# A fused decoder layer on one core: the place of A21's plain product in the up units of the feed-forward

## The chip, the cores and the metric

The kernel runs on one core of a Trainium2 chip. The metric is the device time of one launch in microseconds, the median of three runs.

## What is computed

The reference is one inference step of a one-layer hybrid trunk: a mixer (gated linear attention, a gated linear recurrence and sliding-window attention side by side), cross-attention to a memory, and a feed-forward block, each added to the residual. It is done for 1024 prompt rows and for 8 sample rows. The change lies in the feed-forward block, with a width of 1024 and 4096 hidden features:

```python
def ffn(x, g, w1, w2):
    h = rmsnorm(x, g) @ w1
    return jnp.square(jax.nn.relu(h)) @ w2
...
xp = xp + ffn(xp, g_ffn[l], ffn_w1[l], ffn_w2[l])
...
xs = xs + ffn(xs, g_ffn[l], ffn_w1[l], ffn_w2[l])
```

## The kernel before, in words

Activations lie transposed, features on the partitions and the 1032 rows (1024 prompt, 8 sample) as columns, in three groups of 344. Every float32 operand of a product is split into a high and a low half, and a product is three matmuls for each block of 128 features: high by high, low by high, high by low (`terms`, L1938). `halves` makes the two: ScalarE writes the high half, VectorE subtracts it from the source (line L171 is the helper of every VectorE subtraction or addition, L161 of every ScalarE operation, L141 of every matmul).

**The up stage** multiplies by `ffn_w1`. Of its 16 column pairs, two are done plainly before, and 14 are *up units* (`up_unit`, L2037). A unit takes 256 hidden features, seen as a 2 by 2 array of weight blocks A11, A12, A21, A22. For the first two column groups it uses a scheme of seven products in place of eight: A11 and A12 with two blocks of the input, S2, S1, S4 and S3 (sums and differences of the blocks, by GpSimd, L1918) with sums of the input, and A22 with one more. The third column group gets the four plain products of A11, A12, A21, A22. So one weight operand has one or two products, each of 4 blocks x 3 terms = 12 matmuls of 344 columns: 11 products, 132 matmuls a unit.

The PSUM tiles are called `fa` (A11 and A12, first group), `fb` (S2), `fc` (S1), `fg` (S4), `fd` (S3, and A22 on top of it), and `fe` (the plain ones: one tile for A11 and A12, another for A21 and A22). The sums U = fb + p1 and V = fc + U lie in tile `gc`; the outputs of a unit lie in `hc`. Two cells of `hc` come from `fd`: the cell h11 is `fd` + V, read when S3's product alone is in it, and h10 is `fd` + U, read when A22's product has been added to it:

```python
elif i == S3:
    terms(bank(psC, "fd"), w, XOP[T3], True, False)
    with lift(LIFT_E):
        tt(h[1, 1], ps["fd"], V, ADD)
...
elif i == A21:
    terms(bank(psB, "fe"), w, XOP[GA][:4], True, False)
else:
    terms(ps["fd"], w, XOP[T4], False, True)
    terms(ps["fe"], w, XOP[GA][4:], False, True)
```

So TensorE may add A22's product to `fd` only after VectorE has read `fd` for h11.

**Order.** The order of the products in an up unit is that of the eight numbers in L1860: the loop runs i from 0 to 7, and `seq` gives `range(8)` for an up unit. The same numbers order the preparation of the operands: `prep` (L1921) makes the halves (tile `wop`) five products ahead (`LOOK`), in two alternating rings of three buffers each. At A11's preparation it also issues the next unit's weight load (tile `wraw`) and the four sums (tile `wsum`, one buffer each). Between the products, `bg_run(2)` and, from position 5 on, one entry of `slow` put in the storing of finished hidden features: halves into a ring of three buffers (tiles `hst` and `wsum`), subtractions in place (`hc`, `hpl`), and stores to memory (`hd`). In the last up unit, L2099 also issues loads of the down stage's operands at the positions of S1, S4 and S3. A scheduler with priorities then decides the order of the rows on each engine; `lift` gives a step more priority.

**The down stage** (`down_unit`, 16 units) multiplies by `ffn_w2` with the same scheme. Its order names the operands in `seq`, not by number.

Of the kernel before, what the change touches and what calls it, by code (L numbers as in the profile page):

```python
# [52 lines left out]
def trunk_step(ctx: ExitStack, tc: tile.TileContext, I: dict, O: list):  # L53
# [1803 lines left out]

    A11, S2, S1, A12, S4, A21, S3, A22 = range(8)  # L1860
    B11, T2, B21, T1, T3, B22, T4, GA = range(8)
    NPAIR, NPLAIN, NUNIT = DFF // 256, 2, DFF // 512
    HALF, QU, NOP = N // 2, N // 4, 7
# [533 lines left out]
```

## Time and profile before

| | |
|---|---|
| median of 3 runs | 1407.40 us (1407.39 to 1409.67) |
| the profiled execution | 1409.29 us, span of its records 1407.3 us |
| TensorE busy | 1326.3 us (94% of the span), granted clock 0.98 on the mean |
| VectorE, ScalarE, GpSimd busy | 1017.0, 686.8, 255.1 us |
| up units, from the first `fa` matmul to the first of the down stage | 748.72 to 1069.64 us |

Busy time is an average over stages. What the change is worth has to be read in the up stage, from the waits of TensorE there. Matmuls overlap in the records, so a matmul's row is longer than the step from one to the next. In the rows of a timeline the first number is the start in us from the span's start, the second the duration, and the bracket, where there is one, the idle time of the engine before it and what ended it.

### The profile page before, as it was taken

Reading aid. Unit: us, or ns where it says so; the run is one execution under the profiler, and the core shown is the slowest. Engines: PE = TensorE matmul, PEld = TensorE weight load, DVE = VectorE, ACT = ScalarE, POOL = GpSimd, SP = SyncE. Lnnn points to the kernel's source line nnn. Section 1 sums busy time; section 2 is a strip of 40 time slices with the busy share of each in tenths; the row PEclk is TensorE's granted clock in tenths of the full one; section 3 lists DMA queues with packets and bytes.
Section 4 is the critical chain, followed back from the end, with each engine's and each line's share of the span. In section 5 each row is a group of like instructions: output and inputs, shape, how many; then the busy total and the mean of one; then the engine's idle time right before and its main releaser. Section 6 shows DMA issues by size and latency. Waiting matters only on the chain.

```text
span 1407.3 us, 24488 instructions
## 1 busy us (share of the span) xinstructions
PE 1326.3 (94%) x9251; PEld 1219.1 (87%) x9251; DVE 1017.0 (72%) x1993; ACT 686.8 (49%) x1393; POOL 255.1 (18%) x245
## 2 busy tenths in 40 slices
PE   6999999999997989998999999998999999999998
PEld 4889888777876977887798999998999999999997
DVE  6276787668767673767798887887775577877775
ACT  5265464245476554645665666665665422222221
POOL 3001011400003101020014222242202223223310
PEclk9999999999998899998999999999999999999999
DMA  6114010211101453532243777674659989775624
GB/s 183 46 49 120 9 48 18 65 26 31 51 4 54 135 157 113 155 117 75 66 126 118 276 252 268 236 264 179 232 180 343 336 301 343 266 256 209 228 83 121
DMA packets 181021, 215.87 MB, mean 153 GB/s; under 512 B 26866, under 2 KB 114990, under 8 KB 180888
## 3 DMA queue, kind: packets, MB, share of 16 engines
q1 hardware_dynamic: 180264, 214.01, 45.0%
q8 instruction: 73, 1.20, 0.4%
q0 software_dynamic: 640, 0.30, 0.1%
q14 instruction: 44, 0.36, 0.1%
HBM read 145.28 MB, written 70.06 MB: 153 GB/s over the span
## 4 chain that ended last, share of the span: by engine, by line
PE 73%; DVE 14%; ACT 5%; DMA 3%; issue 3%; SPq 1%; POOL 0%; DVEq 0%; ACTq 0%; POOLq 0%
PE win L141 9%; PE a L141 7%; PE d L141 7%; PE c L141 7%; PE wo L141 6%; PE fe L141 4%; PE b L141 3%; PE fa L141 3%; PE fd L141 2%; PE v L141 2%; PE f L141 2%; PE gx L141 2%; PE fb L141 2%; PE fc L141 2%; PE wmo L141 2%
## 5 line engine op out<-in xcount | busy, mean ns | idle before, releaser
L1918 POOL TENSOR_TENSOR wsum<-wraw 128x512 f32<-128x512 f32 x60 | 81.4, 1357 | 408.0 <-DVE wop L171 374.5
L141 PE MATMUL win<-XL,wh 128*128 128x344 f32 x384 | 127.7, 333 | 0.0
L141 PE MATMUL win<-XH,wh 128*128 128x344 f32 x384 | 127.5, 332 | 0.2 <-ACT xy L161 0.2
L141 PE MATMUL win<-XH,wl 128*128 128x344 f32 x384 | 126.7, 330 | 0.0
L161 ACT ACTIVATE wop<-wraw 128x512 fp32r<-128x512 f32 x104 | 65.3, 628 | 118.5 <-PE b L141 31.3
L161 ACT ACTIVATE wop<-wsum 128x512 fp32r<-128x512 f32 x104 | 65.3, 628 | 110.5 <-PE d L141 29.8
L141 PE MATMUL fe<-XH,wop 128*128 128x344 f32 x448 | 117.4, 321 | 0.0
L161 ACT ACTIVATE wh<-ws 128x512 fp32r<-128x512 f32 x130 | 79.9, 626 | 75.0 <-DMA ws<-in_w_out_dram 21.2
L171 DVE TENSOR_TENSOR wop<-wraw,wop 128x512 fp32r<-128x512 f32 x104 | 93.5, 899 | 27.8 <-ACT wop L161 24.7
L171 DVE TENSOR_TENSOR wl<-ws,wh 128x512 fp32r<-128x512 f32 x130 | 93.0, 727 | 28.0 <-ACT wh L161 23.4
L171 DVE TENSOR_TENSOR wop<-wsum,wop 128x512 fp32r<-128x512 f32 x104 | 80.7, 776 | 17.4 <-ACT wop L161 15.0
L141 PEld LDWEIGHTS fe<-XH,wop 128*128 128x128 f32 x448 | 79.8, 189 | 0.0
L141 PEld LDWEIGHTS win<-XL,wh 128*128 128x128 f32 x384 | 73.1, 190 | 5.2 <-issue 3.9
L141 PEld LDWEIGHTS win<-XH,wl 128*128 128x128 f32 x384 | 73.3, 191 | 3.6 <-issue 2.7
L141 PEld LDWEIGHTS win<-XH,wh 128*128 128x128 f32 x384 | 73.2, 191 | 3.3 <-issue 1.9
L161 ACT ACTIVATE hc<-hc 128x344 f32<-128x344 f32 x126 | 59.9, 487 | 29.0 <-DVE hc L171 27.8
L141 PE MATMUL fe<-XL,wop 128*128 128x344 f32 x224 | 71.8, 321 | 0.0
L141 PE MATMUL a<-XH,wop 128*128 128x258 f32 x352 | 67.6, 283 | 0.0
L141 PE MATMUL wo<-XH,wh 128*128 128x344 f32 x192 | 64.3, 335 | 2.2 <-ACT wh L161 2.2
L141 PE MATMUL wo<-XH,wl 128*128 128x344 f32 x192 | 64.1, 334 | 1.0 <-DVE wl L171 0.9
L141 PE MATMUL wo<-XL,wh 128*128 128x344 f32 x192 | 63.0, 328 | 0.0
L141 PE MATMUL d<-XH,wop 128*128 128x258 f32 x320 | 60.8, 282 | 0.0
(543 smaller groups left out, 4109.4 us busy)
## 6 DMA issues: line engine op xcount, KB each, us to landing
hd<-hst SPq DMA_DIRECT2D x75, 516.0 KB
wraw<-in_ffn_w_dram SPq DMA_DIRECT2D x60, 512.0 KB
hd<-wsum SPq DMA_DIRECT2D x37, 516.0 KB
XH<-hd SPq DMA_DIRECT2D x36, 516.0 KB
XL<-hd SPq DMA_DIRECT2D x36, 516.0 KB
xoph<-hd SPq DMA_DIRECT2D x20, 516.0 KB
xopl<-hd SPq DMA_DIRECT2D x20, 516.0 KB
ws<-in_w_in_dram SPq DMA_DIRECT2D x24, 256.0 KB
```

What stands on the lines that cost most here:

```text
L141: PE.matmul(out, lhsT, rhs, start=start, stop=stop, **kw)
L161: return ACT.activation(out, in_, func, **kw)
L171: return DVE.tensor_tensor(out, a, b, op=op)
L1918: POOL.tensor_tensor(o, a, b, op=op)
```

## The change

One line: the numbers of S3 and A21 are exchanged.

```diff
-    A11, S2, S1, A12, S4, A21, S3, A22 = range(8)
+    A11, S2, S1, A12, S4, S3, A21, A22 = range(8)
```

No instruction is added or removed. Here is TensorE in the second up unit, from the plain product of A21 to the next unit's first `fa` matmul, before. Names carry buffer numbers: `wop_7600` is A21's operand, `wop_7634` S3's, `wop_7655` A22's; `fe_7750` is the plain product of A21 and A22, `fd_7769` the tile of S3. Rows between these go on with the same tiles.

```order
L141 MATMUL fe_7750<-XH_83,wop_7600 128x344
...
L141 MATMUL fd_7769<-xoph_6992,wop_7634 128x344 [waits Activation_49]
...
L141 MATMUL fe_7750<-XH_83,wop_7655 128x344 [waits Activation_49]
L141 MATMUL fe_7750<-XL_84,wop_7655 128x344
L141 MATMUL fe_7750<-XH_83,wop_7655 128x344 [waits DVE_49]
...
L141 MATMUL fd_7769<-XH_83,wop_7655 128x344 [waits DVE_49]
...
L141 MATMUL fa_7827<-XH_83,wop_7685 128x344 [waits Activation_49]
```

And the same place after the change; here `wop_7600` is S3's operand, `wop_7634` A21's:

```order
L141 MATMUL fd_7750<-xoph_6992,wop_7600 128x344 [waits PE_49]
...
L141 MATMUL fe_7772<-XH_83,wop_7634 128x344 [waits Activation_49]
...
L141 MATMUL fd_7750<-XH_83,wop_7655 128x344 [waits DVE_49,Activation_49]
...
L141 MATMUL fe_7772<-XH_83,wop_7655 128x344
...
L141 MATMUL fa_7827<-XH_83,wop_7685 128x344 [waits Activation_49]
```

Before, six `fe` matmuls of A22 stood between S3's last `fd` matmul and A22's first, and the other six behind A22's `fd`. After it, all twelve `fe` matmuls of A21 stand there, and all twelve of A22 follow its `fd`.

VectorE in the same unit, from h01 (`hc` from `fg`) to h11 (the first `hc` from `fd`), before:

```order
L171 TENSOR_TENSOR hc_7325<-fg_7727,gc_6995 128x344 [waits PE_49]
L171 TENSOR_TENSOR wop_7743<-wsum_7327,wop_7743 128x512 [waits Activation_49]
L171 TENSOR_TENSOR wsum_7327<-hpl_6591,wsum_7327 128x516 [waits DMAHW6_49,Activation_49]
L171 TENSOR_TENSOR wop_7763<-wraw_7469,wop_7763 128x512 [waits DMAHW4_49,Activation_49]
L171 TENSOR_TENSOR hpl_6591<-hpl_6591 128x516 [waits DVE_49]
L171 TENSOR_TENSOR hc_7326<-fd_7769,gc_6995 128x344 [waits PE_49]
```

and after the change:

```order
L171 TENSOR_TENSOR hc_7325<-fg_7727,gc_6995 128x344 [waits PE_49]
L171 TENSOR_TENSOR wop_7743<-wsum_7327,wop_7743 128x512 [waits Activation_49]
L171 TENSOR_TENSOR hc_7326<-fd_7750,gc_6995 128x344 [waits DVE_49,PE_49]
L171 TENSOR_TENSOR wsum_7327<-hpl_6591,wsum_7327 128x516 [waits DMAHW6_49,Activation_49]
L171 TENSOR_TENSOR wop_7766<-wraw_7469,wop_7766 128x512 [waits DMAHW4_49,Activation_49]
```

The addition of h11 now stands directly behind the halves of one operand; the store's halves, the halves of the next unit's A12 and the subtraction have moved behind it. In all 14 units one `wop` row stands between h01 and h11 after the change. The two preparations of S3 and A21 change places on ScalarE and VectorE; the rows of the load and store queue keep their order.

## Rows read from the trace of the kernel before

**Rows 1.** The page: busy time, share and instructions of each engine, and the chain that ended last by engine.

```profile
PE 1326.3 (94%) x9251; PEld 1219.1 (87%) x9251; DVE 1017.0 (72%) x1993; ACT 686.8 (49%) x1393; POOL 255.1 (18%) x245
PE 73%; DVE 14%; ACT 5%; DMA 3%; issue 3%; SPq 1%; POOL 0%; DVEq 0%; ACTq 0%; POOLq 0%
```

**Rows 2.** The waits of TensorE from 750 to 1070 us: who waited for whom, us in total, times, longest.

```profile
PE fd L141 <- DVE hc L171: 22.1, 13, 3.7
PE a L141 <- ACT hc L161: 0.5, 1, 0.5
```

**Rows 3.** Busy time by stretch, each stretch one up unit from its first `fa` matmul to the next unit's (units 2, 5, 6, 9 and 13). Columns: the stretch, its length, busy time (and instructions) of PE, PEld, DVE, ACT, POOL, the granted TensorE clock, DMA share, GB/s.

```profile
771.19:793.65 22.46, 21.07 (x134) 20.79 (x133) 18.56 (x27) 15.06 (x31) 5.84 (x4) 1.00 0.67 244
838.67:863.33 24.66, 22.31 (x134) 22.02 (x133) 18.76 (x28) 14.99 (x30) 5.79 (x4) 0.94 0.75 259
863.33:886.13 22.80, 21.41 (x134) 21.12 (x133) 18.37 (x27) 15.00 (x30) 5.84 (x4) 0.99 0.64 232
931.05:957.28 26.23, 22.58 (x134) 22.29 (x133) 20.17 (x24) 14.11 (x29) 12.77 (x8) 0.93 0.59 210
1024.69:1045.73 21.04, 21.04 (x134) 20.79 (x133) 15.46 (x24) 14.01 (x29) 1.30 (x1) 1.00 0.47 177
```

**Rows 4.** The timeline of TensorE: the up stage's first matmul, unit 2's first, and in unit 2 the products of A21 (`fe`), S3 (`fd`) and A22.

```profile
748.72 0.32 PE L141 MATMUL fa<-XH,wop 128*128 128x344 f32 x1
...
771.19 0.32 PE L141 MATMUL fa<-XH,wop 128*128 128x344 f32 x1
...
784.45 0.32 PE L141 MATMUL fe<-XH,wop 128*128 128x344 f32 x1
...
786.32 0.32 PE L141 MATMUL fd<-xoph,wop 128*128 128x344 f32 x1
...
788.06 0.32 PE L141 MATMUL fd<-xoph,wop 128*128 128x344 f32 x1
788.23 0.32 PE L141 MATMUL fe<-XH,wop 128*128 128x344 f32 x1
...
790.72 0.43 PE L141 MATMUL fd<-XH,wop 128*128 128x344 f32 x1 [1.39 <-DVE hc L171]
```

**Rows 5.** The timeline of VectorE in the same unit: two rows near its beginning, and the rows from h01 to h11.

```profile
777.08 0.52 DVE L171 TENSOR_TENSOR gc<-fb,gc 128x344 f32<-128x344 f32 x1
777.74 1.29 DVE L171 TENSOR_TENSOR wop<-wraw,wop 128x512 fp32r<-128x512 f32 x1
...
784.64 0.52 DVE L171 TENSOR_TENSOR hc<-fg,gc 128x344 f32<-128x344 f32 x1 [0.18 <-PE fg L141]
785.31 0.69 DVE L171 TENSOR_TENSOR wop<-wsum,wop 128x512 fp32r<-128x512 f32 x1
786.76 1.16 DVE L171 TENSOR_TENSOR wsum<-hpl,wsum 128x516 fp32r<-128x516 f32 x1 [0.76 <-ACT wsum L161]
787.85 1.78 DVE L171 TENSOR_TENSOR wop<-wraw,wop 128x512 fp32r<-128x512 f32 x1
789.55 0.68 DVE L171 TENSOR_TENSOR hpl<-hpl 128x516 f32<-128x516 f32 x1
790.16 0.50 DVE L171 TENSOR_TENSOR hc<-fd,gc 128x344 f32<-128x344 f32 x1
```

**Rows 6.** The timeline of GpSimd in the same unit.

```profile
777.19 1.30 POOL L1918 TENSOR_TENSOR wsum<-wraw 128x512 f32<-128x512 f32 x1 [6.63 <-DVE wop L171]
786.08 1.29 POOL L1918 TENSOR_TENSOR wsum<-wraw 128x512 f32<-128x512 f32 x1 [7.60 <-DVE wop L171]
787.45 1.62 POOL L1918 TENSOR_TENSOR wsum<-wsum,wraw 128x512 f32<-128x512 f32 x1
```

**Rows 7.** The timeline of TensorE: the stalls in units 5, 9 and 14, and the first matmul of the down stage.

```profile
859.16 0.43 PE L141 MATMUL fd<-XH,wop 128*128 128x344 f32 x1 [2.35 <-DVE hc L171]
...
952.85 0.66 PE L141 MATMUL fd<-XH,wop 128*128 128x344 f32 x1 [3.65 <-DVE hc L171]
...
1066.17 0.43 PE L141 MATMUL fd<-XH,wop 128*128 128x344 f32 x1 [2.13 <-DVE hc L171]
...
1069.64 0.39 PE L141 MATMUL a<-xoph,wop 128*128 128x258 f32 x1 [0.55 <-ACT hc L161]
```

**Rows 8.** The timeline of VectorE in unit 9: h01 and the halves behind it.

```profile
947.06 0.51 DVE L171 TENSOR_TENSOR hc<-fg,gc 128x344 f32<-128x344 f32 x1
947.49 0.68 DVE L171 TENSOR_TENSOR wop<-wsum,wop 128x512 fp32r<-128x512 f32 x1
```

**Rows 9.** The timeline of TensorE in unit 9: the first matmul of S3 and the first behind S3's product.

```profile
946.19 0.32 PE L141 MATMUL fd<-xoph,wop 128*128 128x344 f32 x1
...
948.09 0.32 PE L141 MATMUL fe<-XH,wop 128*128 128x344 f32 x1
```

**Rows 10.** The timeline of ScalarE in unit 14: halves of a store, and the reading of the last `fe` tile.

```profile
1063.53 0.64 ACT L161 ACTIVATE hst<-hc 128x516 fp32r<-128x516 f32 x1 [1.83 <-DMA hd<-hst]
...
1069.13 0.46 ACT L161 ACTIVATE hc<-fe 128x344 f32<-128x344 f32 x1 [1.15 <-PE fe L141]
```

**Rows 11.** The timeline of VectorE in unit 14: h11, and h10 with the row before it.

```profile
1065.61 0.50 DVE L171 TENSOR_TENSOR hc<-fd,gc 128x344 f32<-128x344 f32 x1
...
1068.02 1.01 DVE L171 TENSOR_TENSOR wsum<-hc,wsum 128x516 fp32r<-128x516 f32 x1 [0.70 <-ACT wsum L161]
1068.95 0.50 DVE L171 TENSOR_TENSOR hc<-fd,gc 128x344 f32<-128x344 f32 x1
```

**Rows 12.** Busy time by stretch in the down stage, columns as in Rows 3.

```profile
1100.00:1130.00 30.00, 30.00 (x253) 30.00 (x252) 17.95 (x26) 9.60 (x16) 8.40 (x7) 1.00 1.04 390
1340.00:1370.00 30.00, 30.00 (x253) 30.00 (x252) 24.77 (x38) 6.97 (x11) 5.17 (x4) 1.00 0.19 71
```

## The prediction

> **What bounds the kernel now.** I read the page first, for the engine that sets the time. TensorE is busy for 94% of the span and holds 73% of the chain that ended last, VectorE 14% [rows 1]. So the change is worth what it does to TensorE's idle time and to its clock in the up stage, and the next view is who makes TensorE wait there. From 750 to 1070 us there are two rows: 22.1 us in 13 waits of an `fd` matmul for VectorE's `hc`, and 0.5 us at the first matmul of the down stage [rows 2]. That is all. Third, the length of a unit: unit 2 takes 22.46 us, and unit 13, the one without such a wait, 21.04 us at a granted clock of 1.00 [rows 3]. Both have the same 132 matmuls; the difference of 1.42 us is the stall of 1.39 us and its edges. Fourth, the timelines around that stall. S3's twelve `fd` matmuls start at 786.32 us and the last ends at 788.06 + 0.32 = 788.38 us; six `fe` matmuls follow from 788.23 us; then TensorE stands for 1.39 us until 790.72 us [rows 4]. VectorE reads `fd` for h11 from 790.16 to 790.66 us, 2.28 us after the product was complete [rows 5]. It wasn't waiting for the product: the addition stood in the queue behind a store's halves (1.16 us), the halves of an operand (1.78 us) and a subtraction (0.68 us), back to back from 786.76 us [rows 5].
>
> In the down stage TensorE is busy throughout, 30.00 us of 30.00 at a clock of 1.00 [rows 12]. It starts when the up stage lets it, so what the up stage gains moves the end by as much.
>
> **The change, part by part.** It adds and removes no instruction; it moves 12 matmuls, two preparations and one addition in each of 14 units.
>
> *The cover on TensorE.* Between S3's last matmul and A22's first now stand six `fe` matmuls, afterwards A21's twelve. From one product's start to the next is 786.32 - 784.45 = 1.87 us for twelve [rows 4], so the cover grows from 0.94 to 1.87 us. That alone is less than the 2.28 us by which h11 is late.
>
> *The lateness on VectorE.* After the change h11 stands directly behind h01 and one operand's halves. On unit 2's times: S3's product takes A21's place, starts at 784.45 and is complete near 786.5 us. VectorE is done with h01 and those halves at 785.31 + 0.69 = 786.00 us [rows 5]. So h11 runs from about 786.55 to 787.05 us, and A22's first `fd` matmul, behind A21, is due at 788.23 us. The margin is 1.2 us, and the stall of 1.39 us goes whole. What is late next in that unit is nothing on TensorE: the rows moved behind h11 (1.16 + 1.78 + 0.68 us) feed a store and the next unit's A12, which TensorE takes more than five products later.
>
> GpSimd's sums run at 786.08 and 787.45 us [rows 6], so the addition now falls beside them, while before it stood clear. Does that stretch it? Operand halves beside a sum took 1.29 and 1.78 us in place of 0.69, but `gc` from `fb` took 0.52 us at 777.08 us with a sum running from 777.19 us [rows 5, 6]. h11 is of that second kind, with one input in PSUM. The Trainium skill (SBUF — State Buffer, section Who interferes with whom) says that a VectorE instruction with two SBUF inputs contends with a GpSimd instruction that reads SBUF, and that one with at most one SBUF input does not. The trace agrees: 0.52 us. If h11 were stretched like the halves, by 1.78 - 0.69 = 1.09 us, it would end near 788.14 us, still before 788.23, and the sum would lose nothing in unit 2.
>
> *The plain units.* The 13 stalls sum to 22.1 us; without those of 2.35, 3.65 and 2.13 us [rows 7] ten are left with 14.0 us. I count them whole: **14.0 us**.
>
> *Unit 5.* It takes 24.66 us at a granted clock of 0.94, and unit 6 22.80 at 0.99 [rows 3]: behind the stall of 2.35 us the clock fell from 2.4 to 1.2 GHz for a while. Against 21.04 us and unit 2's 22.46 that is 3.62 + 0.34. Without the stall I take both: **3.9 us**.
>
> *Unit 9.* It takes 26.23 us at 0.93 [rows 3], 5.19 over unit 13. VectorE is behind here: GpSimd has 12.77 us of sums in the unit [rows 3], and the halves behind h01 end only at 947.49 + 0.68 = 948.17 us [rows 8]. h11 would then end near 948.65 us. S3 and A21 would be done when A22 is due, at 948.09 us [rows 9], which leaves a stall of 0.55 us. Stalls of 1.39 us left the clock at 1.00 in unit 2 [rows 3], so I give back only the 0.55: **4.6 us**. Bounds: 5.2 without any stall; 2.2 if the stall is 1.5 us and the clock still falls (3.65 - 1.5).
>
> *Unit 14.* ScalarE waits 1.83 us here for a store to land, until 1063.53 us [rows 10], and VectorE's h11 ends at 1066.11 us [rows 11]. After the change h11 no longer stands behind that store. But the store's own chain stays: from that landing its halves, further halves, h10 (1068.95 us) and ScalarE's reading of the last `fe` tile (1069.13 us) must run before the down stage's first matmul may start in their PSUM banks, at 1069.64 us [rows 7, 10, 11]. Of it only h11's 0.50 us and some waiting leaves. So most of this stall turns up again in front of the down stage: of 2.13 + 0.55 I take **0.8 us**, between 0 and 2.7.
>
> *Costed at nothing.* The exchanged preparations of S3 and A21: both are made five products, over 9 us, ahead of their use. GpSimd's third sum may be written earlier, since S3's halves free its buffer earlier. The last loads of L2099 are released one product sooner; their place in the queue is the same. The load on memory rises by 5% in the up units; their DMA share is 0.47 to 0.75 [rows 3], and 1.04 (390 GB/s) is reached elsewhere [rows 12].
>
> *The sum.* 14.0 + 3.9 + 4.6 + 0.8 = 23.3 us. The profiled execution took 1409.29 us, 2.0 over its span of 1407.3; it would take 1386.0. It stands 1.9 us over the median of the runs, 1407.40, and against that I predict **1384.1 us**. As a check, 14 units of 21.04 us are 294.6 us, and the stage takes 1069.64 - 748.72 = 320.9 [rows 4, 7]. The whole excess is 26.4 us, which no version of this change can exceed; the low end is 1381.0.
>
> **The rivals.** *Only the cover grows.* If VectorE reaches h11 as late behind S3's product as now, because rows queue up in front of h01 instead, each of the 13 stalls shrinks by 1.87 - 0.94 = 0.93 us: 12.1 us, and unit 5's clock with it, 3.9 - 2.35 = 1.6: 13.7 us, 1393.7 us. For it: VectorE is the busiest of the helpers, 18.56 of 22.46 us [rows 3], and would have 88% of a unit of 21.04. Against it: in unit 2 it waited 0.18 us for `fg` itself at h01 [rows 5], so it had caught up. Its chance is 0.11.
>
> *No change.* VectorE, ScalarE and the stores set the length of a unit, and TensorE waits elsewhere, on U, V or an operand. Then a unit keeps its 22.46 us, and the time 1407. Against it: unit 13 ran in 21.04 us, though with 15.46 us of VectorE and few sums [rows 3]; and between h01 and h11 VectorE still had gaps. 0.05.
>
> *Slower.* After the change no matmul of A22 is ahead of its `fd`, so a late h11 stops TensorE with nothing else to do. If VectorE fell behind by what the shorter unit takes from it, h11 could come more than 1.87 + 1.39 = 3.26 us after S3's product; from there each stall is longer than today's. If it were the 2.35 us of unit 5, at which the clock fell, 12 more units would take 24.66 instead of 22.46 us: 26 us more, 1434 us. For it: in unit 9 VectorE began h01 at 947.06 us [rows 8], though S4's product was complete near 946.19 - 1.87 + 0.2 = 944.5 us [rows 9], 2.6 us before. Against it: that took 12.77 us of GpSimd's sums, other units have 5.8 [rows 3]. 0.04.
>
> That the change doesn't do what it says is not among them: the order of rows shows both moves in all 14 units.
>
> **The numbers.** My case has 0.80, with its own range from 1381.0 (all 26.4 us) to 1389.5 (unit 9 at 2.2, unit 14 at nothing, 0.2 us left in each other unit). To hold 8 in 10 the range reaches to the first rival: **1381 to 1394 us**. Both mean faster; a change of 0.2%, 2.8 us, is about what a measurement can tell from none. Faster 0.91, same 0.05, slower 0.04.
>
> **What would show it.** Right: the row of `fd` waiting for `hc` falls from 22.1 us to about 1; up units of 21.0 to 21.2 us at a clock of 1.00; h11 starting within 0.2 us of S3's end; the wait of the first down matmul growing from 0.55 to 1 to 2.5 us. Wrong: stalls of about 0.4 us in each unit (first rival), TensorE waiting at `fb`, `fc`, `fg` or `fa` (second), or stalls over 2 us with a clock under 1 (third).

## The result, and the profile after

The changed kernel takes 1397.3 us in the median of four runs (1395.8 to 1398.8), the kernel before 1407.4. The ratio is 0.9928, with a 95% interval from 0.9909 to 0.9948. So the change is faster by about 10 us, where 23.3 were predicted, and 1397.3 lies outside the range of 1381 to 1394.

The page of the changed kernel, busy time and the chain by engine:

```profile
PE 1324.1 (95%) x9251; PEld 1218.5 (87%) x9251; DVE 1012.9 (73%) x1993; ACT 684.3 (49%) x1393; POOL 259.1 (19%) x245
PE 67%; DVE 15%; DMA 8%; ACT 6%; issue 3%; SPq 1%; POOL 0%; DVEq 0%; ACTq 0%; POOLq 0%
```

Busy times are within 5 us of those of [rows 1]. What is new is the chain: DMA holds 8% of it, 3% before. The waits of TensorE from 750 to 1070 us, as in [rows 2]:

```profile
PE fd L141 <- ACT hc L161: 7.0, 7, 1.7
PE a L141 <- ACT hc L161: 4.1, 1, 4.1
PE fg L141 <- DVE gc L171: 2.6, 1, 2.6
```

The 22.1 us of `fd` waiting for `hc` have become 7.0, not about 1, and two waits stand where there was 0.5 us: 4.1 us in front of the down stage and 2.6 us for `gc`. (The `fd` waits are put down to ScalarE, whose rows on `hc` end 0.02 to 0.03 us after VectorE's h11. They read h01, not `fd`; the wait is still that for h11.) Busy time by unit shows where they are; units 2, 4, 9, 11 and 14, columns as in [rows 3]:

```profile
768.91:789.73 20.82, 20.82 (x134) 20.82 (x133) 16.73 (x25) 14.39 (x29) 5.49 (x4) 1.00 0.73 257
...
811.11:833.90 22.79, 21.06 (x134) 20.81 (x133) 18.90 (x29) 14.88 (x30) 5.87 (x4) 1.00 0.80 279
...
922.25:947.02 24.77, 21.32 (x134) 20.79 (x133) 21.11 (x26) 14.22 (x29) 12.81 (x8) 1.00 0.68 231
...
967.84:988.66 20.82, 20.82 (x134) 20.82 (x133) 16.79 (x25) 14.13 (x29) 6.42 (x4) 1.00 0.66 229
...
1030.53:1055.63 25.10, 20.99 (x135) 20.71 (x133) 16.65 (x26) 15.61 (x32) 3.85 (x3) 0.97 0.87 314
```

Units 2 and 11 run their 132 matmuls without a gap, and no unit of any kernel here is shorter by more than 0.01 us. Unit 4 isn't, and it has 29 VectorE rows where units 2 and 11 have 25. The table sums the up units by group for the kernels of this study. The last unit is taken with the first product of the down stage, which took 3.00 us before and 5.32 after.

| us | units 1, 2 | 3 to 8 | 9 | 10 to 12 | 13 | 14 + first down product | together |
|---|---|---|---|---|---|---|---|
| before | 44.93 | 137.40 | 26.23 | 67.41 | 21.04 | 26.91 | 323.92 |
| changed | 41.64 | 132.52 | 24.77 | 62.46 | 21.05 | 30.42 | 312.86 |
| e_order | 44.51 | 131.82 | 27.20 | 66.11 | 20.93 | 26.82 | 317.39 |
| e_dma | 41.64 | 132.76 | 25.11 | 64.94 | 22.79 | 29.64 | 316.88 |
| e_halves | 41.64 | 132.41 | 24.81 | 67.42 | 22.67 | 30.49 | 319.44 |
| e_last | 41.64 | 132.58 | 26.58 | 62.46 | 20.82 | 26.23 | 310.31 |
| e_slow2 | 41.64 | 131.15 | 22.71 | 68.63 | 21.27 | 29.35 | 314.75 |
| e_late | 41.64 | 133.37 | 21.19 | 62.45 | 23.65 | 30.53 | 312.83 |
| e_loads | 41.64 | 133.11 | 26.70 | 62.46 | 20.82 | 27.91 | 312.64 |
| e_raw | 48.43 | 124.92 | 20.82 | 62.46 | 20.82 | 29.58 | 307.03 |
| e_raw2 | 41.64 | 125.00 | 25.08 | 62.46 | 20.82 | 30.43 | 305.43 |
| e_spread | 41.64 | 133.29 | 22.27 | 62.46 | 21.12 | 28.63 | 309.41 |
| e_thin | 42.47 | 130.68 | 21.48 | 64.43 | 22.77 | 32.46 | 314.29 |
| e_hold | 41.64 | 133.84 | 22.38 | 62.46 | 20.82 | 24.52 | 305.66 |

The stage gained 323.92 - 312.86 = 11.06 us; the profiled executions differ by 12.05 (1409.29 and 1397.24). Lengths of units are compared here rather than whole times wherever a kernel has one run: the first `fa` matmul starts anywhere from 743.8 to 749.1 us in kernels that are the same up to there.

**Where the change did what was predicted.** In unit 2, ScalarE's half for the third of the previous unit's seven stores, then VectorE from a store of the plain pairs (`hpl`) and the previous unit's last store to h11:

```profile
771.31 0.64 ACT L161 ACTIVATE hst<-hc 128x516 fp32r<-128x516 f32 x1
...
780.88 0.70 DVE L171 TENSOR_TENSOR hst<-hpl,hst 128x516 fp32r<-128x516 f32 x1 [0.49 <-ACT hst L161]
...
781.79 0.70 DVE L171 TENSOR_TENSOR hst<-hc,hst 128x516 fp32r<-128x516 f32 x1 [0.21 <-ACT hst L161]
...
783.26 0.51 DVE L171 TENSOR_TENSOR hc<-fg,gc 128x344 f32<-128x344 f32 x1
783.68 0.69 DVE L171 TENSOR_TENSOR wop<-wsum,wop 128x512 fp32r<-128x512 f32 x1
784.28 0.51 DVE L171 TENSOR_TENSOR hc<-fd,gc 128x344 f32<-128x344 f32 x1
```

h11 ends at 784.79 us. A22's first `fd` matmul starts at 785.95 us, 17.04 us behind the unit's first matmul. The margin of 1.16 us is the 1.2 us of the prediction.

**Where it didn't: unit 4.** ScalarE's half for the same third store, then ScalarE, VectorE and TensorE from 822.80 us to A22:

```profile
815.85 0.64 ACT L161 ACTIVATE hst<-hc 128x516 fp32r<-128x516 f32 x1
...
822.80 0.64 ACT L161 ACTIVATE wsum<-hc 128x516 fp32r<-128x516 f32 x1 [1.36 <-DMA hd<-wsum]
...
825.30 0.64 ACT L161 ACTIVATE hst<-hpl 128x516 fp32r<-128x516 f32 x1 [1.52 <-DMA hd<-hst]
...
825.97 0.70 DVE L171 TENSOR_TENSOR hst<-hpl,hst 128x516 fp32r<-128x516 f32 x1 [1.07 <-ACT hst L161]
...
826.88 0.70 DVE L171 TENSOR_TENSOR hst<-hc,hst 128x516 fp32r<-128x516 f32 x1 [0.21 <-ACT hst L161]
...
828.35 0.51 DVE L171 TENSOR_TENSOR hc<-fg,gc 128x344 f32<-128x344 f32 x1
...
828.77 0.68 DVE L171 TENSOR_TENSOR wop<-wsum,wop 128x512 fp32r<-128x512 f32 x1
...
829.37 0.51 DVE L171 TENSOR_TENSOR hc<-fd,gc 128x344 f32<-128x344 f32 x1
...
830.03 0.40 PE L141 MATMUL fd<-XH,wop 128*128 128x344 f32 x1 [1.73 <-ACT hc L161]
```

Between h01 and h11 stands one `wop` row, as the order said. But h01 itself comes late: S4's product was complete at 824.5 us, and h01 starts at 828.35. Ahead of it stands the previous unit's last store (`hst` from `hc`, 826.88), and ahead of that a store of the plain pairs (`hst` from `hpl`, 825.97), for which ScalarE waited 1.52 us until an earlier store had landed and freed its buffer. That last store must come before h11 in any order: `hc` is one pair of tiles for all units (L1996), and the last store reads the first 516 columns of the second tile (`st(T4, c)`, L1970), of which h11 overwrites a part. In unit 11 no plain store stands there:

```profile
981.49 0.70 DVE L171 TENSOR_TENSOR hst<-hc,hst 128x516 fp32r<-128x516 f32 x1 [0.70 <-ACT hst L161]
982.35 0.69 DVE L171 TENSOR_TENSOR wop<-wsum,wop 128x512 fp32r<-128x512 f32 x1 [0.17 <-ACT wop L161]
982.96 0.51 DVE L171 TENSOR_TENSOR hc<-fg,gc 128x344 f32<-128x344 f32 x1
983.39 0.68 DVE L171 TENSOR_TENSOR wop<-wsum,wop 128x512 fp32r<-128x512 f32 x1
983.99 0.51 DVE L171 TENSOR_TENSOR hc<-fd,gc 128x344 f32<-128x344 f32 x1
```

Counted from the unit's first matmul, h11 ends after 15.88 us in unit 2, 16.66 in unit 11 and 18.77 in unit 4, and A22 is due after 17.04. In unit 4 that is 18.77 - 17.04 = 1.73 us too late, and the stall is 1.73 us as well.

A plain store ahead of the last one isn't enough for a stall: unit 2 has one in the same place. What adds to it is the work left over from the unit before. The units became shorter, and the stores didn't move forward with them: counted from unit 2's own first matmul, ScalarE's half for its last store started 33.4 us in before the change and 34.6 us in after it. What no longer fits runs over into the next unit. The third store's half starts 2.40 us into unit 2 (771.31 - 768.91) but 4.74 us into unit 4 (815.85 - 811.11), about 1.9 us in both before; the last store's row on VectorE comes 12.88 us into unit 2 and 15.77 us into unit 4, 11.60 us in both before. The landings make it longer: in units 3 to 8 ScalarE waits for stores to land 18 times, 19.5 us in all, where it waited 6 times, 3.7 us, before the change.

**Unit 9.** GpSimd, VectorE and TensorE up to S4's first matmul:

```profile
932.46 1.80 DVE L171 TENSOR_TENSOR wsum<-hc,wsum 128x516 fp32r<-128x516 f32 x1
...
933.67 1.71 POOL L1918 TENSOR_TENSOR MKV<-wraw,wsum 128x512 f32<-128x512 f32 x1
934.19 1.75 DVE L171 TENSOR_TENSOR wop<-wraw,wop 128x512 fp32r<-128x512 f32 x1
...
935.85 0.50 DVE L171 TENSOR_TENSOR gc<-fb,gc 128x344 f32<-128x344 f32 x1
...
936.41 0.42 PE L141 MATMUL fg<-XH,wop 128*128 128x344 f32 x1 [2.63 <-DVE gc L171]
```

Five sums of GpSimd run in a row from 926.87 to 935.38 us, ending with the one into `MKV`, which is the fourth sum of the first *down* unit. Beside them five rows of VectorE take 1.69 to 1.80 us instead of 0.69, and U (`gc` from `fb`) comes so late that S4's product waits 2.63 us. The Trainium skill (SBUF — State Buffer, section Who interferes with whom) says that a VectorE instruction with two SBUF inputs contends with a GpSimd instruction that reads SBUF. The trace agrees with it: all five rows have two such inputs.

**Unit 14.** ScalarE, VectorE and TensorE in front of the down stage:

```profile
1048.97 0.64 ACT L161 ACTIVATE hst<-hc 128x516 fp32r<-128x516 f32 x1 [2.05 <-DMA hd<-hst]
...
1049.64 0.89 DVE L171 TENSOR_TENSOR hst<-hc,hst 128x516 fp32r<-128x516 f32 x1 [2.40 <-ACT hst L161]
...
1051.96 1.80 DVE L171 TENSOR_TENSOR wsum<-hc,wsum 128x516 fp32r<-128x516 f32 x1
...
1053.68 0.50 DVE L171 TENSOR_TENSOR hc<-fd,gc 128x344 f32<-128x344 f32 x1
1054.22 1.01 ACT L161 ACTIVATE hc<-hc 128x344 f32<-128x344 f32 x2 [2.29 <-DVE hc L171]
1055.14 0.44 ACT L161 ACTIVATE hc<-fe 128x344 f32<-128x344 f32 x1
...
1055.63 0.58 PE L141 MATMUL a<-xoph,wop 128*128 128x258 f32 x1 [4.11 <-ACT hc L161]
```

h11 was early here (1045.88 us), and A22 had no stall. But the unit's own first stores stand in front of h10 (1053.68) and of ScalarE's reading of the last `fe` tile (1055.14), and the first of them waits for a buffer until 1048.97. So the landing that held h11 before holds the down stage now. The clock shows the rest, in windows from 1048 to 1066 us:

```profile
1048.00:1054.00 6.00, 3.52 (x23) 3.23 (x21) 4.23 (x5) 2.17 (x4) 3.17 (x3) 1.00 1.05 390
1054.00:1060.00 6.00, 4.37 (x20) 4.38 (x21) 1.48 (x3) 2.82 (x6) 1.60 (x1) 0.51 1.03 410
1060.00:1066.00 6.00, 6.00 (x48) 6.00 (x47) 3.10 (x5) 2.79 (x5) 0.00 (x0) 0.92 0.43 126
```

After the stall of 4.11 us the granted clock is 0.51, the level of 1.2 GHz.

### The profile page after: what moved, and what is told of

It is laid out like the page before. It is cut to its first block, busy times and chain, and to the rows that moved or that the text cites. A ratio compares the mean times of both kernels' runs of the same rounds, so it can differ in the third digit from the quotient of the medians.

```text
span 1395.5 us, 24502 instructions
## 1 busy us (share of the span) xinstructions
PE 1324.1 (95%) x9251; PEld 1218.5 (87%) x9251; DVE 1012.9 (73%) x1993; ACT 684.3 (49%) x1393; POOL 259.1 (19%) x245
## 4 chain that ended last, share of the span: by engine, by line
PE 67%; DVE 15%; DMA 8%; ACT 6%; issue 3%; SPq 1%; POOL 0%; DVEq 0%; ACTq 0%; POOLq 0%
PE win L141 9%; PE a L141 7%; PE d L141 7%; PE c L141 7%; PE wo L141 6%; PE b L141 3%; PE fe L141 3%; DMA hd<-hst 3%; PE v L141 2%; PE f L141 2%; DMA hd<-wsum 2%; PE gx L141 2%; DVE hst L171 2%; PE fa L141 1%; PE fd L141 1%
## 5 line engine op out<-in xcount | busy, mean ns | idle before, releaser
L1918 POOL TENSOR_TENSOR wsum<-wraw 128x512 f32<-128x512 f32 x60 | 85.4, 1424 | 392.7 <-DVE wop L171 371.1
L171 DVE TENSOR_TENSOR wop<-wraw,wop 128x512 fp32r<-128x512 f32 x104 | 81.3, 782 | 10.4 <-ACT wop L161 10.0
L171 DVE TENSOR_TENSOR hst<-hc,hst 128x516 fp32r<-128x516 f32 x65 | 55.9, 860 | 17.5 <-ACT hst L161 16.0
L161 ACT ACTIVATE hst<-hc 128x516 fp32r<-128x516 f32 x65 | 41.2, 635 | 54.4 <-DVE hc L171 38.9
```

What stands on the lines that cost most here:

```text
L161: return ACT.activation(out, in_, func, **kw)
L171: return DVE.tensor_tensor(out, a, b, op=op)
L1918: POOL.tensor_tensor(o, a, b, op=op)
```

## The experiments

In the edits `mark(key, x)` names an instruction, and `late(y, key)` orders another behind it. The code cuts are shortened; "..." marks what is left out.

**VectorE's order alone** (e_order): the old order of products, with A12's preparation and that position's stores written behind h11.

```diff
 elif i == S3:
...
-        tt(h[1, 1], ps["fd"], V, ADD)
+        mark("h11", tt(h[1, 1], ps["fd"], V, ADD))
+    gate[0] = 3          # the next three rows of VectorE are held behind h11
+    ahead()              # prep, bg_run, slow: written here, not ahead of S3
+    gate[0] = 0
```

> The order of products as before the change (A21, S3, A22); VectorE's halves of the next unit's A12 are held behind the addition of h11, and the preparation and storing of that position are written behind it. Theory 1 (the row in front of h11 on VectorE made the stall, not TensorE's short cover): the stalls of 1.39 us go, in units 2 and 10 to 12 such a unit takes 20.8 to 21.1 us, though only six to nine fe matmuls stand in the gap. Theory 2 (the twelve matmuls of A21 are needed as cover): these units keep at least 0.5 us of stall, 21.5 to 22.5 us. Both: units 3 to 9 stay longer, the whole time is 1395 to 1403 us under theory 1.

1402.7 us beside 1406.1. In units 3 and 4 h11 stands behind one `wop` row, and they take 20.93 us each with TensorE's order as before. Units 2 and 10 to 12, which the expectation named, missed theory 1: they took 22.46 and 22.0 us, theory 2's figures. But in them rows still stand between h01 and h11 (in units 10 to 12 the unit's own first store and a subtraction, in unit 2 a plain store and a subtraction), and stalls of 0.94 and 1.38 us are left, so they test neither theory. Units 6 and 9 took 25.11 and 27.20 us, at granted clocks of 0.93 and 0.87. So what freed units 3 and 4 is that only that one row stands between h01 and h11; the twelve `fe` matmuls as cover were not needed for it there. It bears on the order of VectorE as the change's cause, and doesn't tell why units 3 to 8 fell short.

**Two suspects for units 3 to 8, each added to units 10 to 12.** e_dma sends three of the unit's seven stores (the expectations count six) a second time to scratch memory; e_halves makes the halves of the same three stores twice and sends nothing more.

```diff
 SP.dma_start(d, st.rearrange("p (s c) -> p s c", s=2))
+if 10 <= p < 13 and op in (T1, T3, T2):      # e_dma
+    SP.dma_start(e, st.rearrange("p (s c) -> p s c", s=2))
...
 halves(hi, lo, src)
+if 10 <= p < 13 and op in (T1, T3, T2):      # e_halves
+    halves(hi, lo, src)
```

> The changed kernel, with three of the six stores in units 10 to 12 written twice, the second time to a scratch tensor: nine stores a unit, as in units 1 to 7, with no more work on VectorE or ScalarE. Theory 1 (the landing of stores holds the ring of three buffers, ScalarE waits for it, VectorE behind it, and h11 comes late): units 10 to 12, now 20.82 us each, take 21.3 to 22.8 us, and ScalarE's waits for landings there grow from under 1 us to several. Theory 2 (VectorE has too much to do in units with nine stores): they stay at 20.8 to 20.9 us.

> The changed kernel, with the halves of three of the six stores in units 10 to 12 made twice: three more rows on ScalarE (0.64 us each) and on VectorE (0.69 us) a unit, and no more stores. Theory 1 (landing of stores): units 10 to 12 stay at 20.8 to 21.0 us. Theory 2 (VectorE's work): they take 21.3 to 22.8 us, with TensorE waiting for h11.

Unit 11 in e_dma and in e_halves, columns as before:

```profile
965.82:987.30 21.48, 21.06 (x134) 20.81 (x133) 17.01 (x25) 13.85 (x29) 6.40 (x4) 1.00 0.82 292
```

```profile
967.75:990.14 22.39, 21.05 (x134) 20.80 (x133) 19.01 (x28) 15.28 (x32) 6.41 (x4) 1.00 0.60 213
```

Both lengthen it from 20.82 us: three more transfers by 0.66, three more pairs of halves by 1.57. In units 10 to 12 the stalls are 0.42 to 0.81 us and 1.29 to 1.60 us. The second is near 3 x 0.69 = 2.1 us of VectorE less the margin of 0.38 us that unit 11 had (17.04 - 16.66). Both suspects can do it; the work does more. In both kernels unit 13 grew as well, to 22.8 and 22.7 us, behind one landing of 3.4 and 3.3 us for which ScalarE waited; why that one is so late isn't settled.

**The plain pairs' stores without their halves** (e_raw, and e_raw2 with the transfers held in place).

```diff
 def h_store(p, op, src):
+    if p < NPLAIN:
...
+        for s in range(2):
+            SP.dma_start(d[:, s], src)       # e_raw2: late(..., "unit"), behind h01
+        return
     st = ST["ring"][ST["n"] % len(ST["ring"])]
```

> The changed kernel, with the plain pairs' hidden features sent to memory as they are, twice, without their halves and without the ring of buffers (left out: the split of these features into halves). The bytes moved stay the same. Theory (work of VectorE and ScalarE, and the ring, make units 3 to 8 longer): these units come to 20.8 to 21.3 us, as units 1, 2 and 10 to 12 are now, 5 to 8 us in all less. Rival (it is the transfers' load on memory): they keep 21.5 to 22.8 us.

> The changed kernel, with the plain pairs' hidden features sent to memory as they are, twice, from the places in the units where their halves were made before, without the halves and the ring (left out: the split of these features into halves). In the run before this one such stores went early, into units 1 and 2, so that units 3 to 8 had neither their work nor their transfers. Theory (the work of VectorE and ScalarE, and the ring, make units 3 to 8 longer): with the transfers in units 3 to 8 again, at a DMA share of 0.7 to 0.9, these units take 20.8 to 21.3 us. Rival (the landing of stores under that load): 21.3 to 22.8 us, as in the changed kernel.

e_raw took 1388.4 us and units 3 to 8 fell to 20.82 us each, but it didn't separate the two: the transfers went ahead into units 1 and 2, the DMA share of units 4 to 8 fell to 0.65, and GpSimd's early sums went with them; beside both, and with landing waits of 3.86 and 2.05 us on ScalarE, unit 2 took 27.61 us. e_raw2 does separate them. Its units 4 and 5:

```profile
810.62:831.45 20.83, 20.83 (x135) 20.83 (x134) 17.52 (x26) 13.81 (x29) 6.41 (x4) 1.00 0.80 277
831.45:852.34 20.89, 20.89 (x134) 20.79 (x133) 18.64 (x27) 14.15 (x29) 6.43 (x4) 1.00 0.95 316
```

With DMA shares of 0.80 and 0.95 they have no stall; in units 3 to 8 the shares are 0.76 to 0.95, against 0.65 to 0.88 in the changed kernel. So the load on memory alone isn't what makes units 3 to 8 long. It is the plain pairs' halves: their rows on ScalarE and VectorE, and the turns of the ring of three buffers that they take (ScalarE's waits for landings in these units fell with them, from 19.5 to 9.2 us). Units 3 to 8 took 125.0 us instead of 132.5, and the run 1390.3.

**Thinner stores** (e_slow2: two entries a unit instead of three).

```diff
-            if i > 4:
+            if i > 5:
```

> The changed kernel, with the plain pairs' hidden features stored at two places a unit instead of three, so that the same work lies over more units. Theory (in units 3 to 8 the rows of the stores, on VectorE and ScalarE, are what h11 stands behind): units 3 to 8, now 22.79, 22.35, 21.54, 22.53 and 21.93 us and the like, come nearer to 20.8, by some 0.5 to 1 us each, while units 9 to 12 get some of the work and grow by up to 0.5 us each; in all 0 to 3 us less. Rival (a fixed lateness of VectorE, whatever the stores): units 3 to 8 keep their lengths within 0.2 us on the mean.

1398.0 us. Units 3 to 8 gained 1.4 us, far less than expected, and units 10 to 12 lost 6.2, 4.0 of them in unit 12. The 2.62 us of wait for `gc` moved with GpSimd's early sums from unit 9 to unit 12 (24.80 us). Spreading the same work gains nothing.

**GpSimd's down sums held until unit 13** (e_late).

```diff
-            POOL.tensor_tensor(o, a, b, op=op)
+            ins = POOL.tensor_tensor(o, a, b, op=op)
+            if UNITS[n][0] == "down" and o is s1:
+                late(ins, "sums")            # behind the last up unit's sums
```

> The changed kernel, with GpSimd's sums for the first down unit held until the last up unit's are done, so that unit 9 keeps its own four sums (about 6 us) and not 12.8 us. Theory (unit 9's remaining wait, 2.63 us at fg for gc and 0.82 at fd, comes from VectorE's halves stretched from 0.69 to about 1.75 us beside those sums): unit 9 takes 20.8 to 21.8 us instead of 24.77, and the whole gains 2 to 4 us unless the sums cost it again near the down stage. Rival (unit 9 is late by the stores alone): it keeps 24 us or more.

Units 9 and 13:

```profile
922.48:943.67 21.19, 21.03 (x134) 20.78 (x133) 17.18 (x26) 14.49 (x30) 6.26 (x4) 1.00 0.82 276
...
1006.12:1029.77 23.65, 21.32 (x134) 20.79 (x133) 19.50 (x27) 14.35 (x29) 9.92 (x6) 1.00 0.42 157
```

Unit 9 lost 3.58 us, unit 13 took 2.60 of them back, with the sums. The cost is the sums' and goes where they go in a row. 1396.6 us is no measurable gain.

**The last unit: its order, its loads.** e_last has the old order in unit 14 alone; e_loads spreads that unit's loads of down operands wider.

```diff
-            return range(8)                                              # e_last
+            return (A11, S2, S1, A12, S4, A21, S3, A22) if n == NPAIR - NPLAIN - 1 else range(8)
...
-  for op in {S1: (B11, T2), S4: (B21, T1), S3: (T3, B22)}.get(i, ()):   # e_loads
+  for op in {S1: (B11,), S4: (T2,), S3: (B21,), A22: (T1,)}.get(i, ()):
```

> The changed kernel, but the last up unit keeps the old order (A21, S3, A22). Theory 1 (in the last unit the stall was the landing of stores behind the loads for the down stage, and the change only moved it in front of the down stage, where it is long enough for the clock to fall): the last unit and the first down product take 26.5 to 27.5 us together instead of 30.4, the granted clock stays at 1.00 there, and the time falls by 3 to 4 us, to about 1394. Theory 2 (the tail comes from the down stage's own loads or from the faster units before it): it stays within 1 us of 30.4 us.

> The changed kernel, with the last up unit's loads of down operands spread wider: one each at the products S1, S4, S3 and A22, the other two in the first down unit. Theory (the last store lands late since those loads run beside it, and the wait before the down stage hangs on that landing): the wait of the first down matmul falls from 4.11 us to 1 to 3 us, the clock stays at 2.4 GHz, and unit 14 with the first down product takes 26.5 to 28.5 us instead of 30.4. Rival (ScalarE and VectorE are late by their own work there): 30 us within 0.5. Against both, the later loads may make the second or third down product wait.

e_last took 1394.0 us. Its unit 14 has a stall of 1.06 us at `fd` and 0.92 at the first down matmul, the clock stays at 1.00, and with the first down product it takes 26.23 us instead of 30.42. So in this one unit the change costs 4.2 us. In e_loads the wait of the first down matmul fell from 4.11 to 2.64 us and the sum to 27.9, which supports the late landing; but the clock still fell (0.66 in the first down product), and the later loads are paid in the down stage: from the second down product to the last record it takes 337.0 us, against 334.6 in the changed kernel. In both, unit 9 took near 26.6 us, with 3.9 and 4.1 us of wait for `gc`: the time at which the early sums fall varies from kernel to kernel.

**Both repairs together** (e_spread): e_last's order, and the four down sums held one each behind the sums of four units.

```diff
+            elif UNITS[n - 1][0] == "up":
+                late(ins, ("sums", 10 + j))
```

> The changed kernel with the old order of the products in the last up unit alone, and with GpSimd's four sums of the first down unit held so that one falls in each of units 10 to 13. Theory (the two costs are apart and each is where it was measured): the last unit with the first down product takes 26 to 27 us instead of 30.4, unit 9 takes 21 to 22 us instead of 24.8, units 10 to 13 lose at most 0.5 us each; in all 1388 to 1391 us, 1.1 to 1.4% under the kernel before. Rival (the sums cost their stall wherever they fall): 1392 to 1395 us.

1390.7 us in five runs, a ratio of 0.9884 [0.9866, 0.9903] to the kernel before. Units 10 to 12 stay at 20.82 us with five sums each: a sum alone costs nothing where VectorE has room. Unit 9 took 22.27 us, and its `gc` wait is gone. Unit 14 was a miss: 2.29 us of stall, the clock at 0.93, 28.63 us.

**Stores laid elsewhere** (e_thin: e_spread, with eight of the 22 plain entries in unit 1, three in unit 2 and one in each of units 3 to 13).

```diff
-            if pos > 4:
+            if pos > (-1 if n == 0 else 4 if n == 1 else 6):
```

> The kernel with the old order in the last up unit and the four sums spread (the run before), and with the 22 entries of the plain pairs' storing laid otherwise: eight in unit 1, which stores nothing else, three in unit 2, one in each of units 3 to 13 instead of three in units 1 to 8. Theory (what makes a unit longer is the sum of its stores' rows on VectorE and ScalarE and the ring's landings, with a threshold, since units 10 to 12 without such entries have no wait): one entry a unit stays under the threshold in about half the units; units 3 to 8 take 20.8 to 21.5 us, units 9 to 13 21 to 22, unit 1 up to 1 us more; in all 1386 to 1390 us, 0 to 4 us under the run before. Rival (each entry costs the same wherever it stands, as the run with two a unit suggests): 1389 to 1393 us, as the run before.

1396.7 us, ratio 0.9926 [0.9909, 0.9944]; worse than the run before, and outside the ranges of the theory and the rival. Units 3 to 8 gained 2.6 us against it, units 10 to 13 lost 3.6. In unit 14, where the old order puts h11 behind the unit's own store, the stall was 6.36 us:

```profile
1042.02 0.64 ACT L161 ACTIVATE wsum<-hc 128x516 fp32r<-128x516 f32 x1 [3.28 <-DMA hd<-wsum]
...
1050.25 0.63 ACT L161 ACTIVATE hst<-hc 128x516 fp32r<-128x516 f32 x1 [1.89 <-DMA hd<-hst]
```

Two landings, of 3.28 and 1.89 us, stand in its way.

**The last unit's own stores held** (e_hold): the new order everywhere, the down sums spread, and unit 14's own stores behind ScalarE's reading of the last `fe` tile (the edit holds the first, and the others stay behind it: none runs in unit 14).

```diff
 def h_store(p, op, src):
-    halves(hi, lo, src)
+    ins = act(hi, src, AF.Copy)
+    if p == NPAIR - 1 and op == B11:
+        late(ins, "fe")
+    tt(lo, src, f32(hi), SUB)
...
-                    square_relu(h[1, 2], ps["fe"])
+                    mark("fe", act(h[1, 2], ps["fe"], AF.Relu))
+                    act(h[1, 2], h[1, 2], AF.Square)
```

> The changed kernel, with GpSimd's four sums of the first down unit spread over units 10 to 13, and with the new order in all 14 units, but the last up unit's own stores held behind ScalarE's reading of its last fe tile. Theory (the wait of 4.11 us before the down stage is that of h10 and of that reading behind two of the unit's own stores, whose buffer is late to land): the wait of the first down matmul falls to 0.3 to 1 us, the clock stays at 2.4 GHz, and unit 14 with the first down product takes 24 to 25 us instead of 30.4; unit 9 takes 21 to 22.5 us; in all 1387 to 1390 us, unless the late stores cost a wait in the down stage. Rival (the operands of the first down products are late by the load on memory itself): the wait stays over 2.5 us or comes back at the second or third down product, 1391 to 1395 us.

1386.9 us in five runs, ratio 0.9863 [0.9843, 0.9882]: the fastest here. ScalarE and TensorE in front of the down stage, and unit 14:

```profile
1045.97 0.46 ACT L161 ACTIVATE hc<-fe 128x344 f32<-128x344 f32 x1 [0.32 <-PE fe L141]
...
1046.48 0.39 PE L141 MATMUL a<-xoph,wop 128*128 128x258 f32 x1 [0.55 <-ACT hc L161]
```

```profile
1024.96:1046.48 21.52, 20.98 (x134) 20.70 (x132) 13.37 (x22) 14.80 (x30) 4.16 (x3) 1.00 0.86 299
```

ScalarE now waits for TensorE's `fe`, not for a landing; 0.55 us is left in front of the down stage, as before the change. Unit 14 with the first down product takes 24.52 us. No wait came back later: from the second down product to the last record it takes 334.6 us, and the changed kernel too.

## Why the prediction was wrong

**The cover, and the lateness on VectorE.** Right where it was worked out: unit 2 came out with the margin as computed, 1.16 us. Units 1, 2 and 10 to 12 gained 8.2 us together; the plain term gave their five stalls 7.0. It missed that a unit without a stall takes 20.82 us, not the 21.04 of unit 13 in [rows 3].

**The plain units (14.0) and unit 5 (3.9): the step that failed.** For units 3 to 8 the two held about 10.9 us; measured are 137.40 - 132.52 = 4.9. The prediction argued from unit 2 that h11 would stand behind h01 and one `wop` row, took it that h01 is on time, and multiplied. It followed the rows between h01 and h11, and not the one ahead of h01: the previous unit's last store. The change brings h11 one product forward, and with it the time by which all seven of those stores must be made. In units 3 to 8 the plain pairs' halves take turns of the same ring and the same engines, and in unit 4 the last store comes 2.1 us later in the unit than in unit 11 (15.77 against 13.65 us), and h11 with it (18.77 against 16.66).

What it put at nothing is the work left over: the rows moved behind h11 were held to make nothing late on TensorE, but in the shorter unit the stores run over into the next one and stand ahead of h01 there. Rows that queue up in front of h01 are the first rival's mechanism (chance 0.11); that VectorE, ScalarE and the stores set the length of a unit is the "no change" rival's (0.05). Both came in six units of fourteen. h11 ends 2.1 to 3.5 us behind S3's product in these units, 2.28 in most of them before. The trace of before held one sign of it: in unit 5 h01 started 14.70 us into the unit, 1.2 us later than in units 2 to 4, behind a landing for which ScalarE had waited 1.37 us. e_raw2 shows the cause: without those halves all six units take 20.8 to 20.9 us. The stores' ring stands neither in the sum nor among the terms costed at nothing; the load on memory does, at 5%, where a unit of 21.04 us in place of 22.46 makes it 6.7%.

**Unit 9 (4.6).** Measured 1.5. The term scaled h11's lateness and took U to be in time. GpSimd's early sums still fall in this unit, and the wait went to S4's product, which starts 0.06 us behind U's end (935.85 + 0.50): 2.63 of the 3.65 us came back there, and 0.82 at `fd`. e_late and e_spread show that it is these sums.

**Unit 14 (0.8).** Measured -3.5. The mechanism was named rightly, that the landing's chain ends at the first down matmul, but the size was wrong and the clock was left out. A wait of 1 to 2.5 us was expected, and 4.11 came. Nothing of the 2.13 + 0.55 us left the unit; the buffer came free 18.44 us behind the unit's first matmul instead of 17.80 (1063.53 - 1045.73, [rows 3, 10]), and from there to the first down matmul it took 6.66 us instead of 6.11, one of the halves on the way taking 1.80. After it the clock was at 1.2 GHz for the first down product: 5.32 us instead of 3.00. e_last and e_hold show both.

**The sum.** Against 23.3 us: units 1, 2 and 10 to 12 gave 1.2 more, units 3 to 8 gave 6.0 less, unit 9 3.1 less, unit 14 4.3 less; 23.3 + 1.2 - 13.4 = 11.1, the stage's gain. Of the rivals, "only the cover grows" came nearest in size (1393.7) and, in units 3 to 8, in cause. But its stalls of 0.4 us everywhere didn't come: there were none in units 1, 2 and 10 to 13, and 0.3 to 1.7 us in units 3 to 8. "Slower" came in unit 4 alone of these by more than 0.1 us (22.79 against 22.46 us).

**What stays open.** The halves' rows and the ring's turns in units 3 to 8 weren't taken apart. A ring of four buffers wasn't tried. And e_hold is 10.4 us under the changed kernel in the medians, of which the stage explains 7.2; in the profiled executions the rest lies ahead of the stage (its first matmul at 743.82 us against 748.09), where the two kernels are the same, and isn't explained.

## What to carry to other kernels

When a consumer is moved forward, ask not only what stands directly ahead of it in its queue, but by when everything must be done that reads the buffer it overwrites. When a wait goes, the unit gets shorter and the work of the engines off the critical path does not; what no longer fits runs over into the next unit. So a margin worked out in one unit doesn't hold for those behind it (here no stall in unit 2, 0.34 us in unit 3 and 1.73 in unit 4): follow the left-over rows through a few units before multiplying by their number. And in the last unit before another stage, a stall that is removed inside comes back at the border if the buffers that the next stage needs are freed behind the same late transfer: hold the unit's own stores behind that.

## What the hardware showed

The clock doesn't follow the length of one stall alone. The changed kernel's stall of 1.73 us at unit 4's `fd` and of 2.63 us at unit 9's `fg` left the granted clock at 1.00. In e_hold, 1.85 us in the same place of unit 4 let it fall:

```profile
824.50:827.50 3.00, 1.15 (x8) 1.14 (x8) 2.00 (x5) 2.37 (x5) 1.52 (x2) 1.00 1.01 367
827.50:830.50 3.00, 3.00 (x13) 3.00 (x12) 3.00 (x4) 2.15 (x5) 1.58 (x1) 0.50 1.03 343
830.50:833.50 3.00, 3.00 (x20) 3.00 (x19) 3.00 (x5) 1.39 (x3) 1.62 (x1) 0.93 0.90 290
```

In the second window TensorE does 13 matmuls in 3 us at 0.50, in the third 20 at 0.93, and unit 4 takes 24.44 us instead of 22.79. In e_spread 1.78 us at that place did the same (24.37 us, clock 0.93), and in e_loads 1.74 us left the clock at 1.00. So stalls near 1.8 us in this place cost about 1.5 us more, or nothing; what decides it isn't shown.
